# Argmax gather and scatter-add: output rows written by three indirect transfers according to their count, one of them a copy inside HBM, and a new counting

One core of one Trainium2 chip. HBM is the memory beside the chip's cores, SBUF the core's own memory. The metric is device time in microseconds (us); the kernel before took 1029.41 us (median of 2 runs, 1028.63 to 1030.19).

## The reference

```python
scores: (8, 2048, 2048) float32      values: (8, 2048, 2560) float32
best_j = argmax(scores, axis=2)                      # one target row per source row
gathered = values[b, best_j, :]
out = zeros_like(values); np.add.at(out, (b, best_j), gathered)
```

A row `r` of `out[b]` is therefore `count(b, r) * values[b, r]`, where the count says how often `r` was the argmax. In the fixed draw 6131 of the 16384 rows have count 0, 5875 have count 1 and 4378 have more. A row is 10,240 bytes.

## The kernel before

Per batch: scores in 16 tiles of 128 rows; row maximum on VectorE, sign mask on ScalarE, column sums of the mask with TensorE give the counts. Then 16 output tiles: rows of nonzero count are gathered (rows of count 0 get an index out of bounds and are skipped), scaled by their count, and the whole tile is written densely.

```python
for t in range(NT):                                   # counting
    nc.sync.dma_start(out=s_tile[:], in_=scores[b, t * P:(t + 1) * P, :])
    nc.vector.tensor_reduce(out=negmax[:], in_=s_tile[:], op=max, negate=True, ...)
    nc.scalar.activation(out=mask[:], in_=s_tile[:], func=Sign, bias=negmax[:, 0:1], scale=1.0)
    for c in range(NC): nc.tensor.matmul(out=cnt_chunks[c][:], lhsT=ones_bf[:], rhs=mask[:, ...], ...)
# ... counts transposed to 128 x 16, row list idx_i (out of bounds where the count is 0) ...
for t in range(NT):                                   # output
    v_tile = vbig[:, vslot * H:(vslot + 1) * H]       # 8 slots
    nc.gpsimd.indirect_dma_start(out=v_tile, in_=values_flat[:, :],
        in_offset=IndirectOffsetOnAxis(ap=idx_i[:, t:t + 1], axis=0), bounds_check=B * S - 1, ...)
    # scaled in place by cnt_sb[:, t]: VectorE for t % 8 < 3, else ScalarE
    nc.sync.dma_start(out=out[b, t * P:(t + 1) * P, :], in_=v_tile)
```

Indirect transfers are issued by GpSimd, loads and dense writes by the sync engine (SP). The instruction order on each engine is fixed when the program is built; the builder may depart from source order (in the kernel before, it put 24 score loads in front of the first dense write, where the source has 16). At run time GpSimd's queue is in order: in every trace here it issues its transfers in the built order, and none passes one that waits.

## Time and profile before

| | before |
|---|---|
| time / span of the profiled run | 1029.41 / 1019.3 us |
| bytes moved by DMA | 407.2 MB, 400 GB/s |
| busy: VectorE, ScalarE, GpSimd | 39%, 44%, 15% |

From the page of the kernel before: the DMA rows of the 40 equal slices of the span (tenths of busy share; GB/s), and the two data queues (packets, MB, share of the time of all 16 DMA engines).

```profile
DMA  6999999999999999999999999999999999994998
GB/s 288 368 381 421 416 418 419 405 418 411 419 423 397 422 414 417 422 382 422 411 405 423 393 415 416 422 408 402 418 416 412 402 411 413 416 384 155 420 413 360
...
q1 hardware_dynamic: 36864, 302.01, 71.8%
q0 software_dynamic: 18432, 105.02, 25.7%
```

The two shares add to 97.5%: the DMA engines are full nearly all the time. The table by stages, with one output stage (78 to 149 us) and one counting stage (149 to 200 us). Behind each stretch and its length stand the busy time of each engine in us with its number of instructions, then the granted TensorE clock, the DMA share and GB/s:

```profile
core 0: us, PE busy (x) PEld busy (x) DVE busy (x) ACT busy (x) POOL busy (x), PEclk, DMA share, GB/s
78.00:149.00 71.00, 3.73 (x8) 0.92 (x8) 12.56 (x8) 28.17 (x12) 12.72 (x10) 0.51 1.01 419
149.00:200.00 51.00, 25.09 (x72) 7.46 (x72) 34.42 (x22) 28.02 (x14) 5.93 (x6) 0.58 1.01 414
```

Both kinds of stage run at 414 to 419 GB/s. So bytes are what cost time here. GpSimd's own waits (who, for whom, us in total, times, longest), and then two of its issues in the timeline (start, us, engine, line, operation, idle before):

```profile
POOL vbig L136 <- DVE idx_i L131: 522.4, 8, 68.7
POOL vbig L136 <- DMA out_dram<-vbig: 296.0, 64, 9.7
```

```profile
71.13 0.99 POOL L136 DMA_INDIRECT vbig<-in_values_dram,idx_i  x1 [0.30 <-issue]
72.43 0.99 POOL L136 DMA_INDIRECT vbig<-in_values_dram,idx_i  x1 [0.30 <-issue]
```

GpSimd waits for the row list of a batch and for a free slot (the dense write eight tiles earlier). An issue takes 1.30 us from start to start. In the packet records a 10,240-byte row holds an engine for 385 ns (median), which is 26.6 GB/s per engine, and a skipped row is a 4-byte packet of 9 ns.

### The profile page before, as it was taken

To read this page: it belongs to the slowest core of one execution; us is meant where nothing else is said; L and a number is where in the kernel's file an instruction comes from. 1 tells how busy PE (TensorE), PEld (TensorE's weight loads), DVE (VectorE), ACT (ScalarE), POOL (GpSimd) and SP (SyncE) were. 2 spreads that over 40 slices of the span, in tenths; PEclk is the share of its full clock that TensorE was granted. 3 is DMA by queue.
4 is the path that set the end of the run, shared out by engine and by line. 5 is a ranking of instruction groups with operands and counts; after the bars stand their busy time and mean duration, and the time that the engine had idled before them with its cause. 6 is when DMAs were issued, how large, how long until landed. Compare 5 with 4: busy or idle time off the path is not lost.

```text
span 1019.3 us, 2882 instructions
## 1 busy us (share of the span) xinstructions
PE 224.5 (22%) x640; PEld 66.0 (6%) x640; DVE 400.8 (39%) x244; ACT 450.9 (44%) x209; POOL 148.3 (15%) x133
## 2 busy tenths in 40 slices
PE   0671003610045000640006400172002610032000
PEld 0120000100011000210002100020000200000000
DVE  8983106811088010970119510394104831054010
ACT  0974144652365422763227623375243741442313
POOL 0022200312003110032100320003100122003120
PEclk9965555655566555655556655556555655555555
DMA  6999999999999999999999999999999999994998
GB/s 288 368 381 421 416 418 419 405 418 411 419 423 397 422 414 417 422 382 422 411 405 423 393 415 416 422 408 402 418 416 412 402 411 413 416 384 155 420 413 360
DMA packets 55313, 407.21 MB, mean 400 GB/s; under 512 B 12275, under 2 KB 12275, under 8 KB 12275
## 3 DMA queue, kind: packets, MB, share of 16 engines
q1 hardware_dynamic: 36864, 302.01, 71.8%
q0 software_dynamic: 18432, 105.02, 25.7%
q8 instruction: 5, 0.08, 0.0%
q14 instruction: 12, 0.10, 0.0%
HBM read 301.99 MB, written 167.77 MB: 461 GB/s over the span
## 4 chain that ended last, share of the span: by engine, by line
issue 50%; DMA 46%; DVE 2%; POOL 1%; ACT 0%; POOLq 0%
DMA vbig<-in_values_dram,idx_i 25%; DMA out_dram<-vbig 21%; DVE vbig L145 2%; POOL vbig L136 1%; ACT vbig L153 0%; POOLq L136 0%; POOLq L186 0%; POOL iota_i L50 0%; POOLq L50 0%; POOLq L175 0%
## 5 line engine op out<-in xcount | busy, mean ns | idle before, releaser
L69 DVE TENSOR_REDUCE negmax<-s_tile 128x1 f32<-128x2048 f32 x128 | 289.7, 2279 | 280.8 <-DMA s_tile<-in_scores_dram 280.6
L87 PE MATMUL cnt_psum<-mask,ones_bf 128*1 128x512 bf16 x512 | 211.1, 556 | 700.4 <-ACT mask L78 700.4
L78 ACT ACTIVATE mask<-s_tile,negmax 128x2048 bf16<-128x2048 f32 x128 | 256.2, 2002 | 223.3 <-DVE negmax L69 197.4
L153 ACT ACTIVATE vbig<-vbig,cnt_sb 128x2560 f32<-128x2560 f32 x80 | 194.1, 2426 | 332.8 <-DMA vbig<-in_values_dram,idx_i 332.8
L136 POOL DMA_INDIRECT vbig<-in_values_dram,idx_i x128 | 148.0, 1156 | 837.3 <-DVE idx_i L131 522.4
L145 DVE TENSOR_SCALAR vbig<-vbig,cnt_sb 128x2560 f32<-128x2560 f32 x48 | 74.9, 1561 | 294.5 <-DMA vbig<-in_values_dram,idx_i 294.5
L87 PEld LDWEIGHTS <-ones_bf 128*1 128x1 bf16 x512 | 53.2, 106 | 847.3 <-issue 835.2
L97 DVE COPY counts_row<-cnt_psum 1x512 f32<-1x512 f32 x32 | 19.8, 671 | 4.1 <-PE cnt_psum L87 3.9
L55 DVE MEMSET vbig<- 128x20480 f32 x1 | 17.1, 17125 | 4.2 <-issue 4.2
L103 PE MATMUL cnt_t_psum<-ident,counts_row 1*128 1x1 f32 x128 | 15.2, 223 | 2.7 <-DVE counts_row L97 1.9
L103 PEld LDWEIGHTS cnt_t_psum<-ident,counts_row 1*128 1x128 f32 x128 | 12.8, 174 | 14.2 <-DVE counts_row L97 8.5
L78 ACT ACT_TABLE_LOAD x1 | 1.3, 1283 | 5.8 <-DMA s_tile<-in_scores_dram 5.8
L131 DVE CAST idx_i<-idx_f 128x16 int32<-128x16 f32 x8 | 1.4, 175 | 0.3
L110 DVE TENSOR_SCALAR cnt_sb<-cnt_t_psum 128x16 f32<-128x16 f32 x8 | 1.2, 155 | 0.5 <-PE cnt_t_psum L103 0.5
L122 DVE SCALAR_TENSOR_TENSOR idx_f<-m0big,iota_f 128x16 f32<-128x16 f32 x8 | 1.2, 155 | 0.0
L113 DVE TENSOR_SCALAR m0big<-cnt_sb 128x16 f32<-128x16 f32 x8 | 1.2, 155 | 0.0
L45 DVE MEMSET ones_bf<- 128x1 bf16 x1 | 0.1, 59 | 0.8 <-PEq L175 0.8
L50 POOL IOTA iota_i<- 128x16 int32 x1 | 0.1, 131 | 0.4 <-POOLq L175 0.4
L175 POOL MEMSET const-float32-0.0<- 128x1 f32 x1 | 0.1, 98 | 0.2 <-issue 0.2
L175 POOL MEMSET const-uint8-127<- 128x1 uint8 x1 | 0.1, 119 | 0.0
L175 POOL MEMSET const-bfloat16-1.0<- 128x1 bf16 x1 | 0.1, 113 | 0.0
L52 DVE CAST iota_f<-iota_i 128x16 f32<-128x16 int32 x1 | 0.1, 110 | 0.0
(2 smaller groups left out, 0.2 us busy)
## 6 DMA issues: line engine op xcount, KB each, us to landing
out_dram<-vbig SPq DMA_DIRECT2D x128, 1280.0 KB, 15.5
s_tile<-in_scores_dram SPq DMA_DIRECT2D x128, 1024.0 KB, 12.9
vbig<-in_values_dram,idx_i POOLq DMA_INDIRECT x128, 19.9
```

The costliest lines, as they stand in the source:

```text
L55: nc.vector.memset(vbig[:], 0.0)
L69: nc.vector.tensor_reduce(out=negmax[:], in_=s_tile[:], axis=mybir.AxisListType.X, op=mybir.AluOpType.max, negate=True,)
L78: nc.scalar.activation(out=mask[:], in_=s_tile[:], func=mybir.ActivationFunctionType.Sign, bias=negmax[:, 0:1], scale=1.0,)
L87: nc.tensor.matmul(out=cnt_chunks[c][:], lhsT=ones_bf[:], rhs=mask[:, c * CH:(c + 1) * CH], start=(t == 0), stop=(t == NT - 1),)
L97: nc.vector.tensor_copy(out=counts_row[0:1, c * CH:(c + 1) * CH], in_=cnt_chunks[c][:])
L103: nc.tensor.transpose(out=cnt_t_psum[:, t:t + 1], in_=counts_row[0:1, t * P:(t + 1) * P], identity=ident1[:],)
L110: nc.vector.tensor_scalar_add(cnt_sb[:], cnt_t_psum[:], float(S))
L113: nc.vector.tensor_scalar(out=m0big[:], in0=cnt_sb[:], scalar1=0.0, scalar2=BIG, op0=mybir.AluOpType.is_equal, op1=mybir.AluOpType.mult,)
L131: nc.vector.tensor_copy(idx_i[:], idx_f[:])
L136: nc.gpsimd.indirect_dma_start(out=v_tile, out_offset=None, in_=values_flat[:, :], in_offset=bass.IndirectOffsetOnAxis(ap=idx_i[:, t:t + 1 ...
L145: nc.vector.tensor_scalar(out=v_tile, in0=v_tile, scalar1=cnt_sb[:, t:t + 1], scalar2=None, op0=mybir.AluOpType.mult,)
L153: nc.scalar.activation(out=v_tile, in_=v_tile, func=mybir.ActivationFunctionType.Copy, bias=0.0, scale=cnt_sb[:, t:t + 1],)
```

## The change

The intent: rows of count 1 need no scaling, so they are copied inside HBM with one transfer instead of two; rows of count 0 need no load, so zeros are scattered from a constant tile; only rows of higher count go through SBUF. The payload falls from 407 to 347 MB. Counting is done with maximum, maximum-index and one-hot matmuls on VectorE and TensorE, which frees ScalarE.

```diff
+def copy_rows(nc, out, in_, idx, bound):     # rows HBM to HBM, destination row from idx
+    ...
         for t in range(NT):
-            nc.vector.tensor_reduce(out=negmax[:], ...)            # then Sign, then 4 matmuls
+            nc.vector.max(out=mx[:], in_=s_tile[:])
+            nc.vector.max_index(out=am[:], in_max=mx[:], in_values=s_tile[:])
+            # lo = am & 127, hi = am >> 7, one-hot rows oh_lo (128) and oh_hi (16)
+            nc.tensor.matmul(out=cnt_ps[:], lhsT=oh_lo[:], rhs=oh_hi[:], start=(t == 0), stop=(t == NT - 1))
...
+        one_i = row_list("one", ALU.not_equal, 1.0)       # out of bounds where the test holds
+        zero_i = row_list("zero", ALU.is_gt, 0.0)
+        many_i = row_list("many", ALU.is_lt, 2.0)
         for t in range(NT):
             v_tile = vbig[:, vslot * H:(vslot + 1) * H]
-            gather by idx_i; scale on VectorE or ScalarE; dense write of the tile from SP
+            nc.gpsimd.indirect_dma_start(out=v_tile, in_=values_flat[:, :], in_offset=...many_i[:, t:t + 1]...)
+            writes_out(copy_rows(nc, out_flat[:, :], values[b, t * P:(t + 1) * P, :], one_i[:, t:t + 1], last_row))
+            writes_out(nc.gpsimd.indirect_dma_start(out=out_flat[:, :], out_offset=...zero_i[:, t:t + 1]..., in_=zrow[:]))
+            nc.scalar.activation(out=v_tile, in_=v_tile, func=Copy, bias=0.0, scale=cnt[:, t:t + 1])
+            writes_out(nc.gpsimd.indirect_dma_start(out=out_flat[:, :], out_offset=...many_i[:, t:t + 1]..., in_=v_tile))
```

`writes_out` tells the builder that the writes go to disjoint rows and need no order among themselves. Also: the 80 KB-per-partition `vbig` is now cleared by GpSimd instead of VectorE. Below, the four transfers of a tile are called gather, copy, zeros and staged scatter.

More of the change, by code (lines that the diff above doesn't have):

```diff
@@ L2 @@
+import copy
 from contextlib import ExitStack
@@ L11 @@
 INT32 = mybir.dt.int32
+U32 = mybir.dt.uint32
+ALU = mybir.AluOpType
 P = 128
+def copy_rows(nc, out, in_, idx, bound):
+    eng = nc.gpsimd
+    n, h = in_.shape
+    src = eng.lower_ap_dma(in_, for_indirect_dma=True)[0]
+    dst = eng.lower_ap_dma(out, for_indirect_dma=True)[0]
+    ind = eng.lower_ap_dma(idx, for_indirect_dma=True)
+    dst = copy.replace(dst, dynamic_ap_info=mybir.DynamicAccessPatternInfo(
+        actual_ap=[[h, n], [1, h]], indirect_dim_max_index=out.shape[0],
+        offset_expr=[mybir.DynamicAccessPatternOffsetExpr(
+            aff_expr=mybir.DynamicAccessPatternOffsetExprAffExpr(arg_id=1, kind="IndirectArgId"), coef=h)]))
+    ins = mybir.InstDMACopy(name=nc.get_next_instruction_name(), engine=mybir.EngineType.Pool, queue="qPoolDynamic",
+                            mode="Copy", oob_is_err=False, ins=[src, ind[0], mybir.RegisterAccess(regref=bound.name, dtype=mybir.dt.int32)], outs=[dst])
+    return eng.add_instruction(ins)
 @with_exitstack
@@ L27, with writes_out @@
     NT = S // P
-    CH = min(512, S)
-    NC = S // CH
-    NB = 8
+    last_row = nc.gpsimd.to_reg(B * S - 1)
     BIG = float(1 << 24)
     values_flat = values.rearrange("b s h -> (b s) h")
+    out_flat = out.rearrange("b s h -> (b s) h")
     consts = ctx.enter_context(tc.tile_pool(name="consts", bufs=1))
     spool = ctx.enter_context(tc.tile_pool(name="spool", bufs=7))
-    mpool = ctx.enter_context(tc.tile_pool(name="mpool", bufs=4))
     small = ctx.enter_context(tc.tile_pool(name="small", bufs=4))
-    cntp = ctx.enter_context(tc.tile_pool(name="cntp", bufs=2))
     idxp = ctx.enter_context(tc.tile_pool(name="idxp", bufs=2))
-    psum_c = ctx.enter_context(tc.tile_pool(name="psum_c", bufs=1, space=bass.MemoryType.PSUM))
-    psum_t = ctx.enter_context(tc.tile_pool(name="psum_t", bufs=2, space=bass.MemoryType.PSUM))
-    ones_bf = consts.tile([P, 1], BF16)
-    nc.vector.memset(ones_bf[:], 1.0)
-    ident1 = consts.tile([1, 1], FP32)
-    nc.vector.memset(ident1[:], 1.0)
+    psum_c = ctx.enter_context(tc.tile_pool(name="psum_c", bufs=2, space=bass.MemoryType.PSUM))
     iota_i = consts.tile([P, NT], INT32)
     nc.gpsimd.iota(iota_i[:], pattern=[[P, NT]], base=0, channel_multiplier=1)
-    iota_f = consts.tile([P, NT], FP32)
-    nc.vector.tensor_copy(iota_f[:], iota_i[:])
+    row_f = consts.tile([P, NT], FP32)
+    nc.vector.tensor_copy(row_f[:], iota_i[:])
+    lane_i = consts.tile([P, P], INT32)
+    nc.gpsimd.iota(lane_i[:], pattern=[[1, P]], base=0, channel_multiplier=0)
+    lane_f = consts.tile([P, P], FP32)
+    nc.vector.tensor_copy(lane_f[:], lane_i[:])
+    zrow = consts.tile([P, H], FP32)
+    nc.vector.memset(zrow[:], 0.0)
+    NB = 8
     vbig = consts.tile([P, NB * H], FP32)
-    nc.vector.memset(vbig[:], 0.0)
+    nc.gpsimd.memset(vbig[:], 0.0)
+    def writes_out(ins):
+        tc.declare_no_dep(ins.ins, group="out", reason="disjoint rows")
+        tc.add_to_no_dep_group("out", ins.ins)
     vslot = 0
     for b in range(B):
-        cnt_chunks = []
-        for c in range(NC):
-            cnt_psum = psum_c.tile([1, CH], FP32, name=f"cnt_psum{c}")
-            cnt_chunks.append(cnt_psum)
+        cnt_ps = psum_c.tile([P, NT], FP32)
         for t in range(NT):
@@ L66 @@
             nc.sync.dma_start(out=s_tile[:], in_=scores[b, t * P:(t + 1) * P, :])
-            negmax = small.tile([P, 1], FP32)
-            nc.vector.tensor_reduce(
-                out=negmax[:],
-                in_=s_tile[:],
-                axis=mybir.AxisListType.X,
-                op=mybir.AluOpType.max,
-                negate=True,
-            )
-            mask = mpool.tile([P, S], BF16)
-            nc.scalar.activation(
-                out=mask[:],
-                in_=s_tile[:],
-                func=mybir.ActivationFunctionType.Sign,
-                bias=negmax[:, 0:1],
-                scale=1.0,
-            )
@@ L86 @@
-            for c in range(NC):
-                nc.tensor.matmul(
-                    out=cnt_chunks[c][:],
-                    lhsT=ones_bf[:],
-                    rhs=mask[:, c * CH:(c + 1) * CH],
-                    start=(t == 0),
-                    stop=(t == NT - 1),
-                )
-        counts_row = small.tile([1, S], FP32)
-        for c in range(NC):
-            nc.vector.tensor_copy(
-                out=counts_row[0:1, c * CH:(c + 1) * CH], in_=cnt_chunks[c][:]
-            )
@@ L101 @@
-        cnt_t_psum = psum_t.tile([P, NT], FP32)
-        for t in range(NT):
-            nc.tensor.transpose(
-                out=cnt_t_psum[:, t:t + 1],
-                in_=counts_row[0:1, t * P:(t + 1) * P],
-                identity=ident1[:],
-            )
-        cnt_sb = cntp.tile([P, NT], FP32)
-        nc.vector.tensor_scalar_add(cnt_sb[:], cnt_t_psum[:], float(S))
-        m0big = idxp.tile([P, NT], FP32, name="m0big")
-        nc.vector.tensor_scalar(
-            out=m0big[:],
-            in0=cnt_sb[:],
-            scalar1=0.0,
-            scalar2=BIG,
-            op0=mybir.AluOpType.is_equal,
-            op1=mybir.AluOpType.mult,
-        )
@@ L121 @@
-        idx_f = idxp.tile([P, NT], FP32, name="idx_f")
-        nc.vector.scalar_tensor_tensor(
-            out=idx_f[:],
-            in0=m0big[:],
-            scalar=float(b * S),
-            in1=iota_f[:],
-            op0=mybir.AluOpType.add,
-            op1=mybir.AluOpType.add,
-        )
-        idx_i = idxp.tile([P, NT], INT32, name="idx_i")
-        nc.vector.tensor_copy(idx_i[:], idx_f[:])
+            mx = small.tile([P, 8], FP32)
+            nc.vector.max(out=mx[:], in_=s_tile[:])
@@ new lines @@
+            am = small.tile([P, 8], U32)
+            nc.vector.max_index(out=am[:], in_max=mx[:], in_values=s_tile[:])
+            lo = small.tile([P, 1], U32)
+            nc.vector.tensor_single_scalar(out=lo[:], in_=am[:, 0:1], scalar=P - 1, op=ALU.bitwise_and)
+            hi = small.tile([P, 1], U32)
+            nc.vector.tensor_single_scalar(out=hi[:], in_=am[:, 0:1], scalar=7, op=ALU.logical_shift_right)
+            oh_lo = small.tile([P, P], BF16)
+            nc.vector.tensor_scalar(out=oh_lo[:], in0=lane_f[:], scalar1=lo[:, 0:1], scalar2=None, op0=ALU.is_equal)
@@ new lines, with row_list @@
+            oh_hi = small.tile([P, NT], BF16)
+            nc.vector.tensor_scalar(out=oh_hi[:], in0=lane_f[:, 0:NT], scalar1=hi[:, 0:1], scalar2=None, op0=ALU.is_equal)
+            nc.tensor.matmul(out=cnt_ps[:], lhsT=oh_lo[:], rhs=oh_hi[:], start=(t == 0), stop=(t == NT - 1))
+        cnt = idxp.tile([P, NT], FP32)
+        nc.vector.tensor_copy(cnt[:], cnt_ps[:])
+        def row_list(name, op, c):
+            big = idxp.tile([P, NT], FP32, name=name + "_big")
+            nc.vector.tensor_scalar(out=big[:], in0=cnt[:], scalar1=c, scalar2=BIG, op0=op, op1=ALU.mult)
+            rf = idxp.tile([P, NT], FP32, name=name + "_f")
+            nc.vector.scalar_tensor_tensor(out=rf[:], in0=big[:], scalar=float(b * S), in1=row_f[:], op0=ALU.add, op1=ALU.add)
+            ri = idxp.tile([P, NT], INT32, name=name + "_i")
+            nc.vector.tensor_copy(ri[:], rf[:])
+            return ri
@@ L136 @@
             nc.gpsimd.indirect_dma_start(
-                out=v_tile,
-                out_offset=None,
-                in_=values_flat[:, :],
-                in_offset=bass.IndirectOffsetOnAxis(ap=idx_i[:, t:t + 1], axis=0),
-                bounds_check=B * S - 1,
-                oob_is_err=False,
-            )
-            if t % 8 < 3:
-                nc.vector.tensor_scalar(
-                    out=v_tile,
-                    in0=v_tile,
-                    scalar1=cnt_sb[:, t:t + 1],
-                    scalar2=None,
-                    op0=mybir.AluOpType.mult,
-                )
-            else:
-                nc.scalar.activation(
-                    out=v_tile,
-                    in_=v_tile,
-                    func=mybir.ActivationFunctionType.Copy,
-                    bias=0.0,
-                    scale=cnt_sb[:, t:t + 1],
-                )
-            nc.sync.dma_start(out=out[b, t * P:(t + 1) * P, :], in_=v_tile)
+                out=v_tile, out_offset=None, in_=values_flat[:, :],
+                in_offset=bass.IndirectOffsetOnAxis(ap=many_i[:, t:t + 1], axis=0),
+                bounds_check=B * S - 1, oob_is_err=False)
+            writes_out(copy_rows(nc, out_flat[:, :], values[b, t * P:(t + 1) * P, :], one_i[:, t:t + 1], last_row))
+            writes_out(nc.gpsimd.indirect_dma_start(
+                out=out_flat[:, :], out_offset=bass.IndirectOffsetOnAxis(ap=zero_i[:, t:t + 1], axis=0),
+                in_=zrow[:], in_offset=None,
+                bounds_check=B * S - 1, oob_is_err=False))
+            nc.scalar.activation(out=v_tile, in_=v_tile, func=mybir.ActivationFunctionType.Copy, bias=0.0, scale=cnt[:, t:t + 1])
+            writes_out(nc.gpsimd.indirect_dma_start(
+                out=out_flat[:, :], out_offset=bass.IndirectOffsetOnAxis(ap=many_i[:, t:t + 1], axis=0),
+                in_=v_tile, in_offset=None,
+                bounds_check=B * S - 1, oob_is_err=False))
 _INS = ['scores', 'values']
```

## The prediction

> **What bounds the kernel now.** The DMA engines. The page's slices show the DMA share near 99% and 400 GB/s over the span; the view by stages shows 414 to 425 GB/s from 78 us on, in load and output stages alike. VectorE is 39% busy, ScalarE 44%, GpSimd 15%. 407 MB at 417 GB/s explain 976 of the 1019 us; the rest is the start. In the trace a 10,240 B row holds a DMA engine for 385 ns (median), gathered or written; a skipped (out of bounds) row 9 ns.
>
> **Bytes.** In the given draw 6131 rows have count 0, 5875 count 1, 4378 more. Before: 134.2 MB scores + 105.0 gathered + 167.8 written = 407. After: 134.2 + 60.2 (count 1, HBM to HBM, moved once instead of twice) + 62.8 (zeros) + 2 x 44.8 (staged) = 346.8 MB, 15% less; HBM traffic is unchanged, only the SBUF side saves. At 417 GB/s that is 832 us. Some 128 x 414 tiny packets x 9 ns / 16 engines add 30 us.
>
> **Engines.**
> - VectorE: a reduction over 128x2048 takes 2.28 us. I estimate maximum and maximum-index at that each, plus four small operations of 0.1 to 0.15 us: 5.2 us a tile, 670 us in all, under the DMA time. The first scatter starts after 16 such tiles, at about 95 us instead of 70; only 23 score loads fit in before, so about 35 us of DMA time is lost. The big memset moves to GpSimd; the Trainium skill (SBUF — State Buffer, section SBUF: two separate sides) says that a GpSimd operation and a two-port VectorE operation exclude each other, which may delay the first small VectorE operations.
> - GpSimd: back-to-back issues are 1.30 us apart (0.99 busy + 0.30). Four per tile make 5.2 us, 665 us in all: no limit, except at the end, when no loads are left and the rows need only 4.1 us of DMA a tile. I charge 25 us.
> - ScalarE: 128 x 2.43 = 311 us, less than now. TensorE nearly nothing.
> - Order: the staged scatter waits for its gather and ScalarE, on an in-order queue. The trace shows that instructions were reordered when built (24 score loads before the first output), so I expect later gathers ahead of that scatter, and transfers queued while GpSimd waits.
>
> **Sum.** 832 + 30 + 35 + 25 = 922 us, plus 10 for time over span and some 15 for imperfect overlap: 950 us, a ratio of 1.08. All the saving is on the critical resource. Range 885 to 1065; faster 0.70, same 0.13, slower 0.17.
>
> **What would show it.** DMA bytes 347 MB; DMA share above 90% from 95 to about 850 us; HBM-to-HBM rows at about 385 ns; maximum-index 2.3 us; VectorE about 65% busy, GpSimd 60 to 70%; little GpSimd idle before the staged scatter.
>
> **What would make it wrong.**
> 1. HBM-to-HBM rows take twice 385 ns: nothing in this trace shows such a copy. That adds 145 us and turns the gain into a loss (1060 to 1090).
> 2. GpSimd waits for each tile's gather and ScalarE before it issues the next gather: over 10 us a tile, 1300 us.
> 3. Scatters or the doubly addressed copy cost far more than 1.3 us to issue: at 2 us each, GpSimd alone takes 1024 us.
> 4. The Trainium skill (DMA: Bandwidth & Descriptors, section SWDGE vs HWDGE vs iDMA) says GpSimd writes descriptors into SBUF, where VectorE's two-port mode locks it out; in this trace issues beside VectorE's scaling took 1.7 to 2.0 us. The new VectorE work has hardly any such operation, but if its small ones do it, point 3 follows.

## More of the kernel before

The rounds ran on different chips; the kernel before took 1026.51, 1027.76 and 1031.85 us on three of them (medians of seven runs, of seven, and one run), so a difference of half a per cent between rounds says nothing.

## The result

The changed kernel took 1412.36 us (1412.17 to 1412.54, 2 runs). The ratio to before is 1.373, 95% interval 1.369 to 1.377. (Ratios here are the mean time of one kernel's runs over the mean of the other's in the same rounds, so not quite the ratio of the quoted medians.) The result is correct.

The same lines of its page:

```profile
PE 20.4 (1%) x128; PEld 12.8 (1%) x128; DVE 649.3 (46%) x979; ACT 312.0 (22%) x129; POOL 529.7 (38%) x519
...
DMA  7669999999999789755975555555555555555554
GB/s 303 223 210 345 339 334 359 341 323 345 329 337 349 269 305 359 259 187 188 354 291 172 176 184 194 188 193 183 185 192 190 185 187 192 182 187 190 182 189 150
...
q0 software_dynamic: 73728, 212.81, 44.2%
q1 hardware_dynamic: 18432, 134.23, 25.9%
```

The bytes are as predicted, 212.81 + 134.23 = 347.0 MB. But the engines are now busy for only 70.1% of 1410 us, that is 989 us; 420 us are idle. (The page also prints "HBM read 469.76 MB, written 503.32 MB". That figure counts skipped rows as if they had moved: 134.2 + 2 x 167.8 and 3 x 167.8. The packets are the ones to use.) No compute engine is busy for more than half of the span. When nothing is full, look for a chain of waits. By stages, then GpSimd's waits:

```profile
25.00:100.00 75.00, 2.58 (x15) 1.67 (x16) 75.00 (x115) 0.00 (x0) 0.00 (x0) 1.00 0.60 217
100.00:750.00 650.00, 15.37 (x96) 9.64 (x96) 534.67 (x775) 134.81 (x56) 219.27 (x219) 1.00 0.86 309
750.00:1400.00 650.00, 2.32 (x16) 1.41 (x15) 18.07 (x78) 176.12 (x73) 291.80 (x292) 1.00 0.56 186
```

```profile
POOL out_dram L129 <- ACT vbig L128: 659.6, 126, 14.3
POOL out_dram L30 <- DVE oh_hi L96: 82.3, 1, 82.3
```

This is a wait that the kernel before did not have: before its staged scatter (L129), GpSimd stands for 660 us in total, in 126 of 128 tiles, until ScalarE has scaled that same tile. One such tile in the late stage, in order of time:

```profile
1003.03 1.02 POOL L119 DMA_INDIRECT vbig<-in_values_dram,many_i  x1 [0.31 <-issue]
1004.35 0.99 POOL L30 DMA_INDIRECT out_dram<-in_values_dram,one_i  x1 [0.30 <-issue]
1005.65 1.00 POOL L124 DMA_INDIRECT out_dram<-zrow,zero_i  x1 [0.30 <-issue]
1007.99 2.43 ACT L128 ACTIVATE vbig<-vbig,cnt 128x2560 f32<-128x2560 f32 x1 [6.52 <-DMA vbig<-in_values_dram,many_i]
1010.70 0.98 POOL L129 DMA_INDIRECT out_dram<-vbig,many_i  x1 [4.05 <-ACT vbig L128]
1011.98 1.03 POOL L119 DMA_INDIRECT vbig<-in_values_dram,many_i  x1 [0.31 <-issue]
```

From one gather to the next, 1003.03 to 1011.98, are 8.95 us: 4.96 us until the gathered rows have landed, 2.43 us on ScalarE, 0.28 us to GpSimd, and 1.28 us to issue the scatter. The next gather is issued only after that. In those 9 us the DMA engines have one tile's 1.66 MB to move, which they could do in 4 us at 417 GB/s. In the first stage, where loads compete and the gather lands later, ScalarE handled 56 tiles in 650 us, 11.6 us a tile.

The order in which the program was built shows the same, and the trace has GpSimd's transfers in this order too. GpSimd's queue, with the transfers of two tiles:

```
18 L119 DMACopy vbig<-in_values_dram,many_i     gather of tile t
19 L30  DMACopy out_dram<-in_values_dram,one_i  copy
20 L124 DMACopy out_dram<-zrow,zero_i           zeros
21 L129 DMACopy out_dram<-vbig,many_i           staged scatter of tile t, waits for ScalarE
22 L119 DMACopy vbig<-in_values_dram,many_i     gather of tile t + 1
```

Before the staged scatter of 127 of the 128 tiles there is no gather of a later tile.

### The profile page after: what moved, and what is told of

Read it like the earlier page. It is cut to its first block, busy times and chain, and to the rows that moved or that the text cites. A ratio compares the mean times of both kernels' runs of the same rounds, so it can differ in the third digit from the quotient of the medians.

```text
span 1410.4 us, 2842 instructions
## 1 busy us (share of the span) xinstructions
PE 20.4 (1%) x128; PEld 12.8 (1%) x128; DVE 649.3 (46%) x979; ACT 312.0 (22%) x129; POOL 529.7 (38%) x519
## 3 DMA queue, kind: packets, MB, share of 16 engines
q0 software_dynamic: 73728, 212.81, 44.2%
q1 hardware_dynamic: 18432, 134.23, 25.9%
HBM read 469.76 MB, written 503.32 MB: 690 GB/s over the span
## 4 chain that ended last, share of the span: by engine, by line
issue 63%; POOL 27%; DVE 6%; DMA 1%; ACT 1%; POOLq 1%
POOL out_dram L124 9%; POOL out_dram L30 9%; POOL out_dram L129 8%; DVE am L88 3%; DVE mx L86 2%; POOL vbig L119 2%; DMA vbig<-in_values_dram,many_i 1%; ACT vbig L128 1%; DVE oh_lo L94 0%; DMA s_tile<-in_scores_dram 0%; POOLq L119 0%; DVE oh_hi L96 0%; POOLq L129 0%; POOLq L158 0%; DVE hi L92 0%
## 5 line engine op out<-in xcount | busy, mean ns | idle before, releaser
L128 ACT ACTIVATE vbig<-vbig,cnt 128x2560 f32<-128x2560 f32 x128 | 310.7, 2427 | 978.0 <-DMA vbig<-in_values_dram,many_i 971.4
L129 POOL DMA_INDIRECT out_dram<-vbig,many_i x128 | 124.8, 975 | 670.6 <-ACT vbig L128 659.6
L88 DVE FIND_INDEX8 am<-mx,s_tile 128x8 uint32<-128x2048 f32 x128 | 300.1, 2347 | 0.0
L86 DVE MAX8 mx<-s_tile 128x8 f32<-128x2048 f32 x128 | 289.7, 2278 | 2.1 <-DMA s_tile<-in_scores_dram 2.1
L30 POOL DMA_INDIRECT out_dram<-in_values_dram,one_i x128 | 127.5, 996 | 123.1 <-DVE oh_hi L96 82.3
L119 POOL DMA_INDIRECT vbig<-in_values_dram,many_i x128 | 131.9, 1030 | 39.2 <-issue 38.3
L124 POOL DMA_INDIRECT out_dram<-zrow,zero_i x128 | 127.9, 999 | 39.0 <-issue 39.0
L94 DVE TENSOR_SCALAR oh_lo<-lane_f,lo 128x128 bf16<-128x128 f32 x128 | 35.2, 277 | 0.0
L97 PE MATMUL cnt_ps<-oh_hi,oh_lo 128*128 128x16 bf16 x128 | 20.4, 172 | 828.3 <-DVE cnt L100 407.1
L96 DVE TENSOR_SCALAR oh_hi<-lane_f,hi 128x16 bf16<-128x16 f32 x128 | 30.1, 235 | 0.0
L61 DVE CAST row_f<-iota_i 128x16 f32<-128x16 int32 x1 | 10.5, 10465 | 0.0
```

Of the source, the lines that this page charges most:

```text
L30: return eng.add_instruction(ins)
L86: nc.vector.max(out=mx[:], in_=s_tile[:])
L88: nc.vector.max_index(out=am[:], in_max=mx[:], in_values=s_tile[:])
L94: nc.vector.tensor_scalar(out=oh_lo[:], in0=lane_f[:], scalar1=lo[:, 0:1], scalar2=None, op0=ALU.is_equal)
L96: nc.vector.tensor_scalar(out=oh_hi[:], in0=lane_f[:, 0:NT], scalar1=hi[:, 0:1], scalar2=None, op0=ALU.is_equal)
L97: nc.tensor.matmul(out=cnt_ps[:], lhsT=oh_lo[:], rhs=oh_hi[:], start=(t == 0), stop=(t == NT - 1))
```

## The experiments

Theory A: the in-order queue of GpSimd makes gather, ScalarE and scatter of each tile one chain, and the time is the sum of 128 such chains after the start. Rival B: rows copied inside HBM hold the DMA engines so long that DMA bounds the kernel (the prediction's first warning). Rival C: the new counting.

### A second ScalarE pass (act_twice)

```diff
             nc.scalar.activation(out=v_tile, in_=v_tile, func=Copy, bias=0.0, scale=cnt[:, t:t + 1])
+            nc.scalar.activation(out=v_tile, in_=v_tile, func=Copy, bias=0.0, scale=1.0)
```

> The changed kernel with a second ScalarE pass (scale 1) over each staged tile, result unchanged. Theory A: 2.43 us more in the chain of each of 128 tiles, so about 1412 + 310 = 1720 us. Rival B: ScalarE is 22% busy and has room, so under 1450 us.

One run: 1681.59 us, correct, 269 us more (2.1 us a tile). ScalarE was busy 299 us longer (610.9 instead of 312.0), so 90% of the added pass shows in the time although ScalarE was only 22% busy: it is on the critical path. B would have hidden the pass. The wait for ScalarE grew from 660 to 923 us in total.

### The gathers issued earlier (ahead0, ahead1, ahead4)

The source was restructured so that each gather can be issued LA tiles ahead of its scatter; everything else is the changed kernel (the row lists got a third buffer, the counting of a batch stands in the source before the outputs of the batch before it).

```diff
+    for k in range(LA): gather(k)
+    for k, (b, t) in enumerate(work):                      # 128 tiles
+        if t == 0 and b + 1 < B: lists[b + 1] = count(b + 1)
+        if k + LA < len(work): gather(k + LA)
         copy; zeros; scale; staged scatter                  # of tile k, as before
```

> The changed kernel, with each gather issued four tiles ahead of the scatter that needs it. Theory A (the in-order GpSimd queue waits for gather and ScalarE in every tile): the wait of the staged scatter, 660 us in the changed kernel, falls below 150 us, and the time falls to what the DMA engines need. In the changed kernel the packets took 70.1% of 1410 us, so 989 us of all engines, which gives 1000 to 1050 us. Rival B (rows copied inside HBM slow the DMA so much that it bounds the kernel by itself): the order hardly matters, and the time stays above 1250 us.

> Control: the source of ahead4 with the gathers 0 tiles ahead instead of 4. In the built program 127 of 128 staged scatters then have no later gather in front of them, as in the changed kernel (in ahead4 124 have four). If the order alone makes the difference: about 1410 us again. If something else in the restructured source did it (a third buffer for the row lists, counts traced a batch earlier): near 1007 us.

> The same with each gather one tile ahead. One tile ahead, GpSimd issues the other three transfers of a tile (3.9 us) while the next gather lands and is scaled (5.1 + 2.4 us by the medians of the changed kernel), so it still waits some 3 to 4 us a tile where the queue is long, and about 1100 us come out; if one tile of lead already covers everything, 1010 us.

| kernel | later gathers in front of a staged scatter, as built | time | GpSimd waits for ScalarE |
|---|---|---|---|
| changed | 0 (127 of 128 tiles) | 1412.36 us | 660 us |
| ahead0 | 0 (127 of 128) | 1397.73 us (one run) | 644 us |
| ahead1 | 1 (127 of 128) | 1022.63 us (one run) | 230 us |
| ahead4 | 4 (124 of 128) | 1006.87 us (4 runs), ratio to before 0.980 (0.975 to 0.985) | 10 us |

This settles it. The same transfers, the same bytes and the same engines' work take 391 us less when only the order differs (ahead0 to ahead4), and one tile of lead gives 375 us of it, more than I had expected of one. The control ahead0 shows that the restructuring by itself is worth at most 15 us. (ahead0 and ahead1 were one run each, on another chip than ahead4; the differences are far larger than that.) A stands; B is out as the main cause. ahead4 is some 2% faster than the kernel before, at the edge of what is counted as a difference here.

The wait before the staged scatter in ahead0, then in ahead1:

```profile
POOL out_dram L147 <- ACT vbig L146: 644.3, 126, 14.1
POOL out_dram L146 <- ACT vbig L145: 230.1, 56, 10.4
```

GpSimd's waits in ahead4, and its stages:

```profile
POOL out_dram L146 <- DMA out_dram<-vbig,many_i: 75.3, 36, 3.4
...
POOL out_dram L146 <- ACT vbig L145: 9.8, 7, 4.7
```

```profile
0.00:100.00 100.00, 2.74 (x16) 1.76 (x17) 96.50 (x128) 0.00 (x0) 17.62 (x7) 1.00 0.67 248
100.00:500.00 400.00, 13.75 (x80) 8.32 (x80) 400.00 (x600) 119.88 (x51) 191.61 (x192) 1.00 1.01 406
500.00:750.00 250.00, 4.65 (x32) 2.90 (x31) 152.33 (x254) 89.77 (x37) 143.61 (x144) 1.00 0.92 343
750.00:1000.00 250.00, 0.00 (x0) 0.00 (x0) 0.00 (x0) 101.95 (x42) 175.13 (x176) 1.00 0.86 297
```

From 100 to 500 us the DMA engines are full again, at 406 GB/s, and GpSimd spends some 170 of these 400 us waiting for earlier transfers to land. What is left are the two ends: a start at 248 GB/s, and a tail without loads in which GpSimd issues 176 transfers in 250 us, 1.42 us each or 5.7 us a tile, near the 5.2 us that four unblocked issues take.

### No copy inside HBM (ahead4_staged)

```diff
-        one_i = row_list("one", ALU.not_equal, 1.0)
-        many_i = row_list("many", ALU.is_lt, 2.0)
+        many_i = row_list("many", ALU.is_lt, 1.0)           # rows of any count but 0
...
-        writes_out(copy_rows(...one_i...))
```

> As ahead4, but rows of count 1 are gathered and scattered with the others (no copy inside HBM), 407 MB as in the kernel before. If a row copied inside HBM holds an engine for about 385 ns, this is some 110 us slower than ahead4. If it holds it for about 630 ns (what the mean of 458 ns over all rows of the changed kernel gives, with 390 ns for the others), it is at most 50 us slower, at 1030 to 1070 us. If for more than 770 ns, it is faster than ahead4.

1039.19 us (4 runs), ratio to before 1.011 (1.006 to 1.017): 32 us slower than ahead4 with 60 MB more, and less than the 110 us that equal row times would give. But this edit also takes away one of the four issues of a tile, so the 32 us are not the worth of the copy alone. A later run, fold3_oldcount below, has the copy and three issues as well and takes 888 us; with 21 us taken off for its other counting (measured below with four issues), I estimate the copy at 1039 - 888 - 21 = 130 us where both have three issues. No single pair of runs isolates it.

### What a row copied inside HBM costs (d2d_direct, d2d_8engines, d2d_eight)

These kernels contain nothing but plain copies of `values` to `out`; their results are wrong.

> Wrong on purpose: nothing but plain copies of values to out inside HBM, 168 MB in rows of 10,240 B. At 385 ns a row it takes about 400 us, at 630 ns 650 us, at twice 385 ns 790 us. It shows whether such a copy is slow by itself or only beside the other traffic.

> Wrong on purpose: the plain copies inside HBM of d2d_direct (521 us on 16 engines, 502 ns for each 10,240 B), on 8 of the 16 engines. If the rate of HBM limited d2d_direct (it moved 644 GB/s, reads and writes together), an engine alone is faster now: 385 ns a row, 16384 x 385 / 8 = 790 us. If each engine is slow at such copies by itself: 502 ns a row, 1030 us.

> Wrong on purpose, mends d2d_8engines, which ran on 16 engines after all: plain copies inside HBM whose outermost dimension is 8. Packets should come to 8 engines only (DMA share 50%). If what the 16 engines do at once limits d2d_direct (502 ns for 10,240 B): 385 ns each here, about 790 us. If each engine is slow at such copies by itself: 502 ns, 1030 us.

d2d_direct took 522.82 us (one run): a packet of 40,960 bytes holds an engine for 2010 ns on average, 502 ns per 10,240 bytes. d2d_8engines (514.23 us, one run) missed its purpose: its copies ran on all 16 engines (DMA share 98.9%), with nearly the same numbers (1975 ns a packet, 655 GB/s). d2d_eight ran on eight, and took 789.78 us (one run). The DMA rows of d2d_direct and then of d2d_eight:

```profile
GB/s 302 305 336 308 324 318 318 336 318 318 340 327 327 333 321 324 330 308 343 314 330 327 328 321 327 330 327 321 336 321 336 305 336 311 352 302 321 336 314 248
...
q1 hardware_dynamic: 6144, 167.78, 99.0%
...
HBM read 167.77 MB, written 167.77 MB: 644 GB/s over the span
```

```profile
GB/s 187 216 214 216 216 213 216 216 216 216 216 216 216 216 216 215 216 216 216 216 216 216 216 216 214 217 216 216 216 216 214 216 216 216 216 217 216 214 214 129
...
q1 hardware_dynamic: 8192, 167.79, 49.6%
...
HBM read 167.77 MB, written 167.77 MB: 426 GB/s over the span
```

With eight engines a packet took 1518 ns, 379 ns per 10,240 bytes: full speed. An engine is therefore not slow at such copies; 16 of them at once are, where reads and writes together reach 644 GB/s. The Trainium skill (HBM Reference, section Specifications (TRN2)) gives about 716 GB/s for the stack that two cores share; the runs fit a limit of that kind, at 644 to 655 GB/s, but don't prove where it sits. So the prediction's first warning, a copy at half rate, does not hold as such. These packets hold four rows and are addressed plainly, so they don't show what a single copied row costs.

In ahead4, 98% of all gathered, copied and scattered rows took less than 390 ns from 120 to 500 us, where loads run beside them (mean 389 ns). As 28.3% of the rows are copied ones, nearly all of these ran at the usual speed too. From 750 to 980 us, without loads, the mean was 454 ns and 16% of the rows took over 400 ns; in ahead4_staged, which copies nothing inside HBM, the means of the two stretches are 386 and 402 ns. If the rows of other kinds keep these, the copied rows took about 400 and about 590 ns (an estimate). So copied rows go with the slow rows of the tail, but why they are slow there is not shown. That all engines meet the copied rows of a tile at the same moment is one guess. A limit on the average rate of HBM is not enough: the tail moves some 300 GB/s, or about 380 GB/s if the copied share is counted twice (an estimate), far below 644.

### The counting alone (before_newcount, ahead4_oldcount)

before_newcount is the kernel before with the new counting; ahead4_oldcount is ahead4 with the old counting (and six score buffers instead of seven). The edits are abbreviated.

```diff
-            tensor_reduce on VectorE; Sign on ScalarE; 4 matmuls          # before_newcount
+            max; max_index; lo; hi; two one-hot rows; 1 matmul
```

```diff
-            max; max_index; lo; hi; two one-hot rows; 1 matmul            # ahead4_oldcount
+            tensor_reduce on VectorE; Sign on ScalarE; 4 matmuls
```

> The kernel before with only the counting changed (maximum, maximum-index, one-hot matmuls); gathers, scaling and dense writes stay. VectorE then needs about 5.1 us a tile instead of 2.28 us, and the first gather comes near 100 us instead of 70 us. If the new counting costs only this later start: 1029 + 30 = about 1060 us. If it is also behind the loss of the whole change: well above 1100 us. If it is free: 1029 us.

> As ahead4 (1007 us), with the counting of the kernel before. The first scatter can start about 50 us earlier, because VectorE has 2.3 us a tile instead of 5.1 us. If the slow start is what ahead4 still loses: 955 to 980 us. If GpSimd's issues are (512 of them, 1.42 us apart at the end of ahead4): they then take 727 us after a start near 60 us, and DMA binds before; again under 985 us. If ScalarE, now with the sign pass again in its in-order queue, delays the staged tiles: no gain or a loss.

before_newcount: 1122.66 us (4 runs), ratio 1.092 (1.090 to 1.094), three times the loss I expected. In the kernel before, SP's queue alternates 16 loads and 16 dense writes, so VectorE's time is not only paid at the start but whenever loads have to wait for it: a load stage, 196 to 250 us, ran at 333 GB/s, and the six full load stages after the first took SP 50 to 61 us from first issue to last, 35 to 37 us in the kernel before. In the changed kernel SP has loads only, and this coupling is gone.

ahead4_oldcount: 986.09 us (4 runs), ratio 0.959 (0.958 to 0.961), 21 us better than ahead4, less than the 27 to 52 us I had expected. The old counting puts a pass of its own on ScalarE, and GpSimd waited 124 us for ScalarE's scaling here instead of 10: that can be why the gain is smaller, but no run separates it. The new counting (rival C) costs some 20 us there: it is not what made the changed kernel slow, and it is no gain either.

### Three transfers a tile (after_fold, fold3_oldcount)

The zero rows need no transfer of their own: the staged scatter can write them, since their tile rows are multiplied by the count 0 (the slots hold finite old rows or the first zeros).

```diff
-        zero_i = row_list("zero", ALU.is_gt, 0.0)
+        rest_i = row_list("rest", ALU.is_equal, 1.0)        # every row whose count is not 1
...
-        writes_out(zeros scattered from zrow by zero_i)
...
-        writes_out(v_tile scattered by many_i)
+        writes_out(v_tile scattered by rest_i)
```

> The changed kernel in its own source order, with the zero rows written by the staged scatter (three transfers a tile). The builder's order then has a later gather in front of 64 of the 128 staged scatters, and of none in the changed kernel. If the order is what counts, two tiles share one wait: 5 us less in every second tile or more, about 1050 to 1150 us. If the number of transfers or of skipped rows counts, with the wait unchanged: above 1300 us.

> As ahead4_oldcount, with the zero rows written by the staged scatter (their tile rows are scaled by the count 0) instead of a scatter of their own: three indirect transfers a tile instead of four, same payload of 347 MB. GpSimd's share falls by a quarter, skipped rows by about 18,000. If GpSimd's issue bounds the end of ahead4: 20 to 50 us faster than ahead4_oldcount. If the DMA engines bound everything: at most 12 us faster (18,000 x 9 ns / 16).

after_fold applies this to the changed kernel in its own source order: 1229.78 us (one run). It missed my range (1050 to 1150), but it is 183 us faster, and the trace shows what changed: two gathers are now followed by one long wait, then the second staged scatter goes out at once. GpSimd waits for ScalarE 100 times instead of 126, for 633 us. Here the order changed only because the builder chose another one; it mixes two effects (order and number of transfers), and I rest nothing more on it.

fold3_oldcount applies it to ahead4_oldcount: 888.33 us (4 runs, 886.38 to 892.57), correct, ratio to before 0.865 (0.862 to 0.868). That is the best kernel, and 98 us faster than ahead4_oldcount, twice what I had expected. Its DMA rows:

```profile
DMA  8999999999999999999969999999999999999997
GB/s 331 369 421 419 422 423 423 423 424 422 422 409 412 403 395 412 422 422 421 411 283 353 401 400 393 340 394 373 376 388 402 402 402 403 392 376 384 359 362 283
```

In the second half, without loads, it moves 385 GB/s (480 to 870 us) where ahead4_oldcount moves 318 (480 to 960 us). Per tile GpSimd takes 390 us x 3 / 272 issues = 4.3 us instead of 480 x 4 / 369 = 5.2 us. In ahead4_oldcount these 5.2 us are just what four issues take; three would take 3.9 us, and the DMA share of 1.00 in that stretch of fold3_oldcount says that DMA binds there instead. The rows are faster too (mean 409 ns instead of 446 ns); why is not shown.

## Why the prediction was wrong

It said 950 us (885 to 1065) and gave 0.17 to a loss; measured were 1412 us.

- **The bound before, and the bytes after: right.** DMA was full at 97.5%; 347.0 MB moved as predicted (346.8).
- **VectorE's estimate: right.** Maximum 2.28 us, maximum-index 2.35 us; 649 us busy against 670 estimated; first output transfer at 100.6 us against 95. A delay of the first small operations was there too: the Trainium skill (SBUF — State Buffer, section SBUF: two separate sides) says that a GpSimd operation and a two-port VectorE operation exclude each other. In the changed kernel, beside GpSimd's clearing of `vbig`, two small casts took 10.5 and 8.2 us (the first of them 0.11 us before), and both ended within 0.2 us after the clearing did at 18.27 us. That agrees with the page; which ports the casts used the trace doesn't show.

```profile
L71 POOL MEMSET vbig<- 128x20480 f32 x1 | 17.2, 17155 | 0.0
...
L61 DVE CAST row_f<-iota_i 128x16 f32<-128x16 int32 x1 | 10.5, 10465 | 0.0
L65 DVE CAST lane_f<-lane_i 128x128 f32<-128x128 int32 x1 | 8.2, 8193 | 0.0
```

- **Issue cost on GpSimd: right.** 1.30 us from start to start also for scatters and for the doubly addressed copy. The Trainium skill (DMA: Bandwidth & Descriptors, section SWDGE vs HWDGE vs iDMA) says VectorE in two-port mode keeps GpSimd from writing descriptors; L30, L119 and L124 averaged 0.996 to 1.03 us, and their medians are the same from 100 to 450 us, with VectorE busy throughout, as from 1000 to 1350 us, with VectorE nearly idle. So the new VectorE work does not do it here.
- **The step that failed** is the sentence "so I expect later gathers ahead of that scatter, and transfers queued while GpSimd waits". The premise was true, that the builder reorders; the inference from SP's loads to GpSimd's gathers was not. (Why the builder left this queue in source order is not shown.) The built queue had a later gather ahead of 1 staged scatter in 128, GpSimd waited 660 us for ScalarE, and the four operations of a tile ran as a chain of 9 to 11.6 us. The prediction named exactly this as its second way to be wrong, with 1300 us, and gave it too little weight. ahead0 and ahead4 put the price of the order at 391 us.
- **A term that was mis-sized**: with the order mended, the rest of the prediction would have been 57 us off (ahead4: 1007 us). The tail without loads was charged 25 us. In ahead4 the last score load came at 622 us already, and from 600 to 1000 us GpSimd issued 277 transfers, so some 69 of the 128 tiles fell into the tail. DMA moved 303 GB/s there; at the 417 GB/s of the sum that stretch would have been 400 x (1 - 303/417) = 109 us shorter. Four issues a tile account for part of it, slower rows (454 ns on average from 750 to 980 us, and not 385) for another.

## What to carry to other kernels

When a queue is in order and one of its instructions waits for work that the same queue started, count how many starts of later work stand in front of that wait in the built program; with none, the latencies add up tile after tile, however idle the engines are. Write the lead into the source order rather than trust a scheduler with it: one tile of lead was worth 375 us here. Saving bytes pays only after that, and then the number of issued transfers is the next price: the three-transfer version with lead, and with the old counting, reached 888 us.

## What the Trainium skill lacked or had wrong

- DMA: Bandwidth & Descriptors has copies between HBM tensors only in a row about large row pitches, and no rate for contiguous ones: here 27.0 GB/s per engine on 8 engines (379 ns for 10,240 bytes), 322 to 327 GB/s in all on 16 (494 to 502 ns); for single rows mixed with loads about 400 ns (an estimate).
- HBM Reference gives about 716 GB/s for a stack, but not how much of it one core reaches with copies inside HBM: 644 to 655 GB/s here, reads and writes together.
- DMA: Bandwidth & Descriptors, in its table of where the fixed 2 us go, calls descriptor generation "small, variable"; its table of latencies has about 1 us to the first byte on GpSimd's path, as the overhead of writing descriptors, which is nearer to the runs. An indirect transfer of 128 rows kept GpSimd for 0.98 to 1.03 us on average in the changed kernel, whatever its direction, and back-to-back issues were 1.30 us apart from start to start.
- The same page does not say what a skipped row costs: one 4-byte packet of 9 ns, and nothing saved on GpSimd (an issue took 0.99 us in the kernel before, with 37% of the rows skipped, and 1.03 us for the gathers of the changed kernel, with 73%; medians).
- VectorE: DVE Perf Modes gives no duration for maximum and maximum-index: 2.28 and 2.35 us for 2048 float32 per partition, plus 0.08 us to load the values to match.
- No page says what the builder does to the order on GpSimd: in the changed kernel, with four transfers a tile, a later gather went ahead of 1 of 128 staged scatters; in after_fold, with three, of 64.
